# First layer's attention: fp32 operands on the two halves of the tensor engine in place of split ones on all of it

## The chip, the cores and the metric

The kernel runs on one core of a Trainium2 chip. The metric is the device time of one execution in microseconds (us); a kernel's time is the median of several. The engines of a core run side by side, each through its own queue: TensorE (PE; its weight loads are listed as PEld), VectorE (DVE), ScalarE (ACT), GpSimd (POOL), and SyncE (SP), which issues transfers.

## The reference, cut to what matters

The program is three transformer layers over 512 tokens of width 1024; the last ends in a mixture of experts. The change is in the mixer of the first, which runs two kinds of attention, each with 8 heads of width 64, over the same normalized input:

```python
# 'fox': causal, with a decay per head
logits = einsum('bqhd,bshd->bhqs', qb, k) * scale + cq[..., None] - cum_k[:, :, None, :]
p = masked_softmax(logits, causal); out = einsum('bhqs,bshd->bqhd', p, v)
# 'dsa': keys picked by an index score, top 128 of each query
rel = relu(einsum('bqhd,bsd->bqhs', qi, k_idx)); score = einsum('bqhs,bqh->bqs', rel, wi)
_, idx = lax.top_k(score, n_keep)
logits = (q_abs . c_sel + q_rot . kr_sel) * scale
p = masked_softmax(logits, valid); out = (p @ c_sel) @ w_uv
```

Queries go in four blocks i = 0..3 of 128; block i sees keys 0 to (i+1)*128. `n_keep` is min(256, 512 // 4) = 128, so block 0 needs no scores. The kernel holds the dsa keys and values per head, made from `ckv` by w_uk and w_uv, so that both kinds have the same shape of work, the dsa logits with a keep mask in place of the causal one.

## The kernel before, in words

**Precision.** A product that must be nearly fp32 is made of three fp32r passes (`mm3`, L317 to L319: hi*hi, hi*lo, lo*hi). Each operand is split as it leaves PSUM: ACT copies the high part, then DVE subtracts it to get the low one (`split_evac`, L310/L311 and L313/L314). Weights are split in the same way, `whi` by ACT (L267), `wlo` by POOL (L280) or DVE (L282).

**Heads.** Two heads share one [128, 512] tile of transposed queries, one on rows 0 to 63, one on rows 64 to 127. Their keys lie in `kd`, one column block for each head with zeros in the other head's 64 rows (`evac_diag`), so each head's logits are a 128-row product. `P` transposed goes to `PTh` (ACT, L633) and `PTl` (DVE, L637); P times values is `mm3` with 64 columns of values as the weight, 128 columns of P at a time. In the fox heads the decay is added to the logits by one more matmul over 8 rows (L1028).

**Stages of layer 0**, in the order of the program: small projections; the dense product for the index queries; the query product (`dense_T`), whose gaps in the code take the index scores (24 items: three blocks by 8 heads, `idx_item`); the key product and the value product, among whose pieces the 48 top-k rounds on DVE are spread (L975, L976); the product for the dsa queries (`qtok2`); `out_proj`.

**The pipeline.** The attention is 40 items (`softmax_item`), 5 for each of 8 pairs of heads, fox first. `Pipeline.step` emits, for step n, each part of an item by its lag, in the order that `SM0` lists: pv of item n-6, T (transposes, L626) of n-4, max (DVE, L606) of n-1, hi of n-5, norm of n-3, qk of n, lo of n-5, out of n-7, exp of n-2. Each engine runs its queue in that order. Steps 0 to 6 are interleaved with the qtok2 product, steps 7 to 35 stand alone (with a top-k round each at first), the last 11 are interleaved with `out_proj`. The preparation of dsa heads (`prep_pair`, `prep_v`) is hung in ahead of steps 15, 19, 21, 26, 29 and 30.

Of the kernel before, what the change touches and what calls it, by code (L numbers as in the profile page):

```python
# [26 lines left out]
SM0 = [('pv', 6), ('T', 4), ('max', 1), ('hi', 5), ('norm', 3), ('qk', 0), ('lo', 5), ('out', 7), ('exp', 2)]  # L27
# [21 lines left out]
NCOLS = 8  # L49
# [37 lines left out]
def tile_kernel(ctx: ExitStack, tc: tile.TileContext, I, out, stage=None, start=None):  # L87
# [489 lines left out]
    def softmax_items(sched, parts, qk, in1, v, out, gate=None):  # L577

        items = []
        for n, part in enumerate(parts):
            later = {h for p in parts[n + 1:] for h, _ in p}
            items.append(softmax_item(sched, part, qk, in1, v, out, {h for h, _ in part} - later, gate))
        return items

    def softmax_item(sched, segs, qk, in1, v, out, ended, gate, parts=None):
# [9 lines left out]
        def s_qk():  # L598
            st["s"] = ps(128, w)
            qk(st["s"], [(h, i, a) for (h, i), a in zip(segs, at)])  # L600

        def s_max():
            st["nm"] = att.tile([128, 2], F32, tag="nm", name="nm", bufs=4)
            st["p"] = att.tile([128, S], F32, tag="P", name="P", bufs=PBUF)
            for c, ((h, i), a) in enumerate(zip(segs, at)):
                nc.vector.tensor_tensor_reduce(st["p"][:, a], st["s"][:, a], in1(h, i), 1.0, 3e38, ALU.add, ALU.min,  # L606
                                               st["nm"][:, c:c + 1])
# [20 lines left out]
        def s_hi():  # L628
            if parts:
                (nc.vector.tensor_copy if parts[3] else nc.scalar.copy)(parts[0]()[:, :w], st["t"])  # L630
                return
# [7 lines left out]
        def s_pv():  # L639
            if parts:  # L640
                return parts[1]()
            for (h, i), a in zip(segs, at):
                o, empty, use = out(h)
                pv([(h, i)], [a], o(), v, st["h"], st["l"], empty, use is not None)

        def s_out():
            if parts:
                return parts[2]()
            for h in sorted(ended):
                o, _, use = out(h)  # L650
                if use:
                    use(o())

        fs = dict(pv=s_pv, T=s_T, qk=s_qk, hi=s_hi, max=s_max, exp=s_exp, norm=s_norm, lo=s_lo, out=s_out)
# [10 lines left out]
    def qk_pairs(q, k, extra=None):  # L665

        def qk(s, segs):
            for h, i, a in segs:
                w = (i + 1) * 128
                ii = slice(i * 128, w)  # L670
                (qh, ql), (kh, kl) = q(h), k(h)
                mm3(s[:, a], qh[:, ii], ql[:, ii], kh[:, h % 2, :w], kl[:, h % 2, :w], True, extra is None)
                if extra:
                    extra(s[:, a], h, i)
        return qk
# [169 lines left out]
    def layer_0():  # L845
# [13 lines left out]
        kd = []  # L859
        for f in range(4):  # L860
            kd.append(tuple(att.tile([128, 2, S], F32R, name=f"kd{f}{c}") for c in range(2)))
            for a in kd[-1]:
                nc.gpsimd.memset(a[0:64, 1].bitcast(F32), 0.0)
                nc.gpsimd.memset(a[64:128, 0].bitcast(F32), 0.0)
# [29 lines left out]
        dense_tok(352, KD, uh, ul, use_small, begun=begun)  # L894
        def small_T():
            for c in range(2):
                split_evac(ckT[0][:, c], ckT[1][:, c], blocks_T(smt, c * 128), cols[:, C_KV + c:C_KV + c + 1])
            evac_diag(kd[0], blocks_T(smt, 256))
            split_evac(rT[0:16], rT[32:48], blocks_T(smt, 384, 16))
# [3 lines left out]
        ck = att.tile([128, 2, S], F32R, name="ck")  # L903
# [3 lines left out]
        def decay_rows():  # L907
# [16 lines left out]
            for g in range(2):  # L924
                nc.scalar.activation(ck[:, g], cmask, AF.Identity, scale=0.0, bias=cols[:, C_DK + g:C_DK + g + 1])
# [6 lines left out]
            for g in range(2):  # L932
                nc.gpsimd.dma_start(ck[4 * g::32, g], ch[g::2])
                nc.gpsimd.dma_start(ck[4 * g + 1::32, g], cl[g::2])
                nc.gpsimd.dma_start(cq[4 * g + 2::32], nh[g::2])
                nc.gpsimd.dma_start(cq[4 * g + 3::32], nl[g::2])
# [3 lines left out]
        dense_tok(512, KD, uh, ul, rope_tok(qtok), after(1, small_T, decay_rows))  # L940
        qi = []

        def turn_qi():
            qi.append(pair_tiles("q", 4))
            split_evac(*qi[-1], blocks_T(qtok, (len(qi) - 1) * 128))
        score = [None] + [att.tile([128, (i + 1) * 128], F32, name=f"score{i}") for i in (1, 2, 3)]

        def idx_item(i, h):
# [3 lines left out]
            def s_qk():  # L952
                st["s"] = ps(128, w)
                qh, ql = (a[:, i * 128:(i + 1) * 128] for a in qi[h // 2])
                mm3(st["s"], qh, ql, kd[0][0][:, h % 2, :w], kd[0][1][:, h % 2, :w], True, True)

            def s_relu():
                st["r"] = att.tile([128, S], F32, tag="P", name="relu", bufs=PBUF)
                nc.scalar.activation(st["r"][:, :w], st["s"], AF.Relu)

            def s_acc():
                r, sc, wt = st["r"][:, :w], score[i], wi[:, i, h:h + 1]
                if h == 0:
                    nc.vector.scalar_tensor_tensor(sc, r, wt, cmask[:, 512 - w:], ALU.mult, ALU.subtract)
                else:
                    nc.vector.scalar_tensor_tensor(sc, r, wt, sc, ALU.mult, ALU.add)
            return [(0, s_qk), (1, s_relu), (2, s_acc)]

        scoring = Pipeline([idx_item(i, h) for i in (1, 2, 3) for h in range(8)])
# [19 lines left out]
        def some_scores():  # L989
            for _ in range(3):  # L990
# [3 lines left out]
        q_b = []  # L994

        def pair_out(lst, tag, scale, bufs):
            def use(f, p):
                lst.append(pair_tiles(tag, bufs))
                split_evac(*lst[-1], p, scale)
            return use  # L1000

        def v_half():
            return tuple(att.tile([128, NT, 256], F32R, tag="t4", name="v" + s, bufs=T4) for s in "hl")

        dense_T(512, KD, uh, ul, pair_out(q_b, "q", -SCALE, 4),
                fine=after(QF0[0], *[turn_qi] * 4, *[some_scores] * QF0[1]))
        dense_T(512, KD, uh, ul, lambda f, p: evac_diag(kd[f], p), fine=spread_topk(TK0[0]))
        vb = [v_half(), v_half()]

        def v_b(t, p):  # L1010
            for a in range(2):
                split_evac(vb[a][0][:, t], vb[a][1][:, t], p[:, a * 256:(a + 1) * 256])
# [4 lines left out]
        def o_out(f):  # L1017

            def place(h):
                c, hs = f + h // 2, hslice(h)  # L1020
                return lazy(lambda: ps(64)), True, lambda o: split_evac(oT[0][hs, c], oT[1][hs, c], o)
            places = [place(h) for h in range(8)]
            return lambda h: places[h]

        def decay(s, h, i):
            r = slice(h // 2 * 32, h // 2 * 32 + 8)
            w = (i + 1) * 128
# [7 lines left out]
        parts = [[(h + a, i) for a, i in part] for h in range(0, 8, 2) for part in PARTS]  # L1035
        items += softmax_items(SM0, parts, qk_pairs(lambda h: q_b[h // 2], lambda h: kd[h // 2], decay),
                               lambda h, i: cmask[:, 384 - i * 128:], values(vb), o_out(4))


        q_a, va = {}, {}  # L1040
        uk_uv = []

        def prep_pair(f):
            def emit():
                if not uk_uv:
                    uk_uv.append(next_unit(1))
                q_a[f] = pair_tiles("q", 4)
                split_evac(*q_a[f], blocks_T(qtok2, f * 128), -SCALE)
# [5 lines left out]
                evac_diag(kd[f], p)  # L1054
            return emit

        def prep_v(a):
            def emit():
                if len(uk_uv) < 2:
                    uk_uv.append(next_unit(1))  # L1060
                va[a] = v_half()
# [9 lines left out]
        items += softmax_items(SM0, parts, qk_pairs(lambda h: q_a[h // 2], lambda h: kd[h // 2]),  # L1071
                               lambda h, i: keep[i], values(va), o_out(0))
# [6 lines left out]
        while attend.at < len(parts):  # L1079
# [6 lines left out]
                 lambda: [rooms(f"kd{f}{c}", 1, 1)[0] for f in range(2) for c in range(2)], oT)  # L1086
# [3 lines left out]
    def layer_1():  # L1090
# [244 lines left out]
        def halves_mm(o, at, of, start=False, stop=False):  # L1335
# [984 lines left out]
```

## Time and profile before

| | |
|---|---|
| median of 3 runs | 2206.71 us (2206.43 to 2208.38) |
| the profiled execution | 2204.43 us, its span 2202.7 us |
| mean granted TensorE clock | 0.982 |
| PE busy | 2105.9 us, 96% of the span |
| DVE, ACT, POOL busy | 1179.6, 848.6, 437.9 us |
| the stages that the change touches | from 84.9 to about 345 us |

Times in views are us from the first instruction of the profiled execution. The span is from its first to its last instruction; the execution's own time is 1.7 us more. In a row of the timeline the first number is the start, the second the duration; matmuls overlap in the pipeline, so the distance from start to start is what one costs. A granted clock of 1.00 is 2.4 GHz, 0.50 is 1.2 GHz.

### The profile page before, as it was taken

The page shows a single profiled execution, that of the slowest core. Times are in us where ns is not written, and L with a number is a line of the kernel's source. Part 1 is how long each engine was busy: PE and PEld are TensorE (multiplying, and loading weights), DVE is VectorE, ACT ScalarE, POOL GpSimd, SP SyncE. Part 2 cuts the span into 40 slices and gives each one's busy share as a digit, 9 for nine tenths or more (in the row PEclk, how much of TensorE's full clock was granted, in tenths as well). Part 3 has the DMA queues.
Part 4 walks back from the last instruction along what each step waited for, and adds up shares of the span by engine and source line. Part 5 has one row for each costly group of instructions (what it writes and reads, how often), then busy time and mean ns, then how long its engine had stood idle before and what let it go on. Part 6 is the DMA issues. An engine that isn't in the chain of part 4 may idle for free.

```text
span 2202.7 us, 29776 instructions
## 1 busy us (share of the span) xinstructions
PE 2105.9 (96%) x11223; PEld 1569.0 (71%) x11223; DVE 1179.6 (54%) x2385; ACT 848.6 (39%) x1624; POOL 437.9 (20%) x564
## 2 busy tenths in 40 slices
PE   7999999999999989999999999989888999999997
PEld 6877788888888877888888887777767444444443
DVE  5587654588684557734778775563755132212223
ACT  4524663344343356743434444553753010101000
POOL 4333241000001345530000002454353000000000
PEclk9999999999999999999999999999999999999999
DMA  4221022532314210022342322302015999999995
GB/s 133 69 77 49 1 68 77 162 115 86 115 39 122 76 50 2 2 87 92 110 134 68 114 80 72 100 16 86 20 67 212 403 409 409 409 409 409 408 408 204
DMA packets 118835, 328.65 MB, mean 149 GB/s; under 512 B 10604, under 2 KB 12716, under 8 KB 118688
## 3 DMA queue, kind: packets, MB, share of 16 engines
q1 hardware_dynamic: 115888, 318.87, 40.1%
q0 software_dynamic: 2800, 7.84, 1.2%
q8 instruction: 90, 1.47, 0.3%
q14 instruction: 57, 0.47, 0.1%
HBM read 324.49 MB, written 2.11 MB: 148 GB/s over the span
## 4 chain that ended last, share of the span: by engine, by line
PE 55%; DVE 5%; POOL 2%; ACT 1%; issue 1%; DMA 0%; DVEq 0%; POOLq 0%; ACTq 0%
PE ps L2019 16%; PE ps L404 10%; PE ps L347 9%; PE ps L743 5%; PE ps L1990 3%; PE ps L2086 2%; PE ps L1337 2%; PE ps L626 2%; PE ps L1353 2%; DVE sl L1725 1%; POOL wlo L280 1%; PE ps L318 1%; POOL sh L1721 1%; PE ps L319 0%; DVE w L1709 0%
## 5 line engine op out<-in xcount | busy, mean ns | idle before, releaser
L267 ACT ACTIVATE whi<-raw 128x1024 fp32r<-128x1024 f32 (+2 forms) x162 | 168.3, 1042 | 358.5 <-PE ps L404 153.3
L280 POOL TENSOR_TENSOR wlo<-raw,whi 128x512 fp32r<-128x512 f32 (+1 forms) x132 | 169.1, 1303 | 390.6 <-ACT whi L267 362.0
L2019 PE MATMUL ps<-ew,xt 128*64 128x512 f32 x1024 | 229.9, 597 | 0.0
L282 DVE TENSOR_TENSOR wlo<-raw,whi 128x1024 fp32r<-128x1024 f32 (+2 forms) x96 | 116.6, 1215 | 207.3 <-ACT whi L267 207.0
L404 PE MATMUL ps<-oTl,whi 128*128 128x512 f32 (+2 forms) x576 | 211.4, 371 | 1.4 <-DVE oTl L311 1.4
L404 PE MATMUL ps<-oTh,whi 128*128 128x512 f32 (+2 forms) x576 | 211.6, 371 | 0.5 <-ACT oTh L310 0.5
L404 PE MATMUL ps<-oTh,wlo 128*128 128x512 f32 (+2 forms) x576 | 166.6, 370 | 0.0
L2019 PEld LDWEIGHTS ps<-ew,xt 128*64 128x64 f32 x1024 | 69.4, 137 | 128.2 <-issue 118.9
L347 PE MATMUL ps<-whi,uTh 128*128 128x512 f32 (+2 forms) x384 | 152.0, 397 | 5.3 <-ACT uTh L310 3.2
L347 PE MATMUL ps<-whi,uTl 128*128 128x512 f32 (+2 forms) x384 | 147.9, 386 | 2.9 <-DVE uTl L311 2.9
L347 PE MATMUL ps<-wlo,uTh 128*128 128x512 f32 (+2 forms) x384 | 118.9, 388 | 6.4 <-POOL wlo L280 6.2
L404 PEld LDWEIGHTS ps<-oTl,whi 128*128 128x128 f32 x576 | 108.5, 188 | 20.8 <-DVE oTl L311 2.1
L404 PEld LDWEIGHTS ps<-oTh,whi 128*128 128x128 f32 x576 | 108.5, 188 | 19.7 <-ACT oTh L310 1.0
L2019 PE MATMUL ps<-ew,hid 128*64 128x512 f32 x512 | 118.4, 600 | 0.7 <-ACT hid L2039 0.7
L404 PEld LDWEIGHTS ps<-oTh,wlo 128*128 128x128 f32 x576 | 104.8, 188 | 18.7
L694 DVE TENSOR_TENSOR x<-ps,x 128x512 f32<-128x512 f32 x124 | 82.0, 684 | 67.0 <-PE ps L347 40.1
L445 POOL DMA_DIRECT2D room<-gains x5 | 2.9, 574 | 566.5 <-DVE fwlo L289 283.4
L613 ACT ACTIVATE P<-P,nm 128x512 f32<-128x512 f32 (+2 forms) x192 | 106.1, 555 | 11.6 <-DVE nm L606 10.4
L606 DVE CUSTOM_DVE_ANT_0 P<-ps,cst 128x128 f32<-128x128 f32 (+3 forms) x168 | 75.0, 473 | 35.1 <-POOL P L621 17.7
L2067 POOL CAST pick<-cst 32x128 fp32r<-32x128 f32 x16 | 4.9, 307 | 442.5 <-PE ps L2074 442.5
L2029 ACT ACTIVATE silu<-ps 128x512 f32<-128x512 f32 x16 | 9.6, 597 | 212.8 <-PE ps L2019 212.8
L347 PEld LDWEIGHTS ps<-wlo,uTh 128*128 128x128 f32 x384 | 72.7, 193 | 24.1 <-POOL wlo L280 10.8
(553 smaller groups left out, 5002.0 us busy)
## 6 DMA issues: line engine op xcount, KB each, us to landing
ew<-w SPq DMA_DIRECT2D x384, 512.0 KB, 10.2
raw<-mlp_w SPq DMA_DIRECT2D x80, 512.0 KB, 3.8
fraw<-mlp_w SPq DMA_DIRECT2D x48, 512.0 KB, 5.6
raw<-w_in SPq DMA_DIRECT2D x24, 512.0 KB, 3.8
raw<-ab_w_in SPq DMA_DIRECT2D x20, 512.0 KB, 3.6
raw<-c_w_in SPq DMA_DIRECT2D x12, 512.0 KB, 3.6
raw<-ab_w_out SPq DMA_DIRECT2D x8, 512.0 KB, 3.8
raw<-c_w_out SPq DMA_DIRECT2D x8, 512.0 KB, 3.7
```

Of the source, the lines that this page charges most:

```text
L267: nc.scalar.activation(hi[:, :w], raw[:, :w], AF.Copy)
L280: nc.gpsimd.tensor_tensor(lo[:, h], raws[r][:, h], hi[:, h], ALU.subtract)
L282: nc.vector.tensor_tensor(lo[:, :w], raws[r][:, :w], hi[:, :w], ALU.subtract)
L347: nc.tensor.matmul(p, a[:, tt], w[:, k], start=u == 0 and n == 0, stop=u == nk - 2 and n == 5)
L404: nc.tensor.matmul(p[:, tt], w[:, k, ff], b[:, u + k, tt], start=start and n == 0, stop=u == nk - 2 and n == 5, **kw)
L606: nc.vector.tensor_tensor_reduce(st["p"][:, a], st["s"][:, a], in1(h, i), 1.0, 3e38, ALU.add, ALU.min, st["nm"][:, c:c + 1])
L613: nc.scalar.activation(p, p, AF.Exp, scale=-1.0, bias=st["nm"][:, c:c + 1], accum_out=st["sm"][:, c:c + 1])
L626: nc.tensor.transpose(st["t"][:, j:j + 128], st["p"][:, j:j + 128], ident)
L694: nc.vector.tensor_tensor(xs, p, xs, ALU.add)
L743: nc.tensor.matmul(acc[b][t], p[:, 2 * h + k, tt], v[:, k], start=begins and h == 0 and m == 0, stop=m == 5, skip_group_check=True)
L1990: nc.tensor.matmul(v, htok[a][:, t, c * 128:(c + 1) * 128], oo[q][:, t], start=t == 0 and a == 0, stop=t == NT - 1 and a == 1)
L2019: nc.tensor.matmul(p[n][half(b)], xs[:, half(b)], w[b][:, n * 512:n * 512 + 512], start=k == 0, stop=k == nk - 1)
```

## The change

`mm3`, the splits of queries, keys, values and P, and the zero-padded `kd` go out of this attention. Operands are plain fp32 copies. `two_rows` makes the logits of a pair by two fp32 matmuls, one with the 64 rows of each head, into two PSUM banks; the fox decay is added in the same way (`decay`), its rows now spread over the pair's 64-row halves. `two_columns` makes P times values by two fp32 matmuls whose 64 weight columns lie on the two halves of the columns. The index scores go by pairs too: 12 items in place of 24. A pair still takes 5 items, but they are cut otherwise: head 0 and head 1 with block 3, head 0 and head 1 with blocks 2 and 0, both heads with block 1 (`two_heads`); the logits of both heads are emitted with the first head's item, the products with the second's. The copy of transposed P is one copy: on ACT for the first head's items, on DVE for the others; `lo` is gone from `SM0`. The output of a pair is split once, not once for each head.

```diff
-SM0 = [('pv', 6), ('T', 4), ('max', 1), ('hi', 5), ('norm', 3), ('qk', 0), ('lo', 5), ('out', 7), ('exp', 2)]
+SM0 = [('pv', 6), ('T', 4), ('max', 1), ('hi', 5), ('norm', 3), ('qk', 0), ('out', 7), ('exp', 2)]
...
-    def softmax_item(sched, segs, qk, in1, v, out, ended, gate, parts=None):
+    def softmax_item(sched, segs, qk, in1, gate, place, take, use, on_vector):
...
-            st["s"] = ps(128, w)
-            qk(st["s"], [(h, i, a) for (h, i), a in zip(segs, at)])
+            st["s"] = qk(segs, at)
...
-            st["h"], st["l"] = (att.tile([128, S], F32R, tag="PT" + c, name="PT" + c, bufs=3) for c in "hl")
-            nc.scalar.activation(st["h"][:, :w], st["t"], AF.Copy)
-        def s_lo():
-            if not parts:
-                nc.vector.tensor_tensor(st["l"][:, :w], st["t"], st["h"][:, :w], ALU.subtract)
...
+            (nc.vector.tensor_copy if on_vector else nc.scalar.copy)(place()[:, :w], st["t"])
+        fs = dict(pv=take, T=s_T, qk=s_qk, hi=s_hi, max=s_max, exp=s_exp, norm=s_norm, out=use)
...
+    def two_rows(dst, of, start=True, stop=True):
+        for c in range(2):
+            nc.tensor.matmul(dst[c], *of(c, slice(c * 64, c * 64 + 64)), start=start, stop=stop)
+    def two_columns(o, at, of, start=False, stop=False):
+        for c in range(2):
+            nc.tensor.matmul(o[c * 64:c * 64 + 64, at], *of(c), start=start, stop=stop, skip_group_check=True,
+                             tile_position=(0, c * 64))
...
+        def pair_tile(tag, bufs, p, scale=1.0):
+            a = att.tile([128, S], F32, tag=tag, name=tag, bufs=bufs)
+            nc.scalar.activation(a, p, AF.Copy, scale=scale)
+            return a
+        def keys(lst, p):
+            f = len(lst)
+            if f % 2 == 0:
+                room_k.append(att.tile([128, 2, S], F32, tag="kd", name="kd", bufs=4))
+            lst.append(room_k[-1][:, f % 2])
+            nc.scalar.activation(lst[f], p, AF.Copy)
+        room_k = []
...
+                st["s"] = [ps(128, w) for _ in range(2)]
+                two_rows(st["s"], lambda c, r: (qi[f][r, i * 128:w], ki[0][r, :w]))
...
-        dense_T(512, KD, uh, ul, lambda f, p: evac_diag(kd[f], p), fine=spread_topk(TK0[0]))
-        vb = [v_half(), v_half()]
+        dense_T(512, KD, uh, ul, lambda f, p: keys(k_b, p), fine=spread_topk(TK0[0]))
...
+            nc.scalar.copy(vb[t // 2][:, t % 2], p)
...
-        def decay(s, h, i):
-            r = slice(h // 2 * 32, h // 2 * 32 + 8)
-            w = (i + 1) * 128
-            nc.tensor.matmul(s, cq[r, i * 128:w], ck[r, h % 2, :w], start=False, stop=True,
-                             tile_position=(h // 2 * 32, 0))
-        def values(vt):
-            return lambda h, j: tuple(a[:, j, h % 4 * 64:h % 4 * 64 + 64] for a in vt[h // 4])
+        def decay(f, s, i, w):
+            two_rows(s, lambda c, r: (cq[r, i * 128:(i + 1) * 128], ck[r, f, :w]), False)
...
+        def two_heads(f, q, k, extra, in1, v, to):
+            o = lazy(ps)
+            new = lambda: att.tile([128, S], F32, tag="PT", name="PT", bufs=6)
+            nothing = lambda: None
+            out, begun = [], []
+            def logits(part):
+                s = [ps() for _ in range(2)]
+                w = 0
+                for i in part:
+                    n = (i + 1) * 128
+                    dst = [a[:, w:w + n] for a in s]
+                    two_rows(dst, lambda c, r: (q()[r, i * 128:n], k()[r, :n]), stop=extra is None)
+                    if extra:
+                        extra(f, dst, i, n)
+                    w += n
+                return s
+            def products(i, p):
+                for j in range(i + 1):
+                    two_columns(o(), slice(i * 128, i * 128 + 128), lambda c: (v(2 * f + c, j), p(c)[:, j * 128:j * 128 + 128]),
+                                not begun, j == i)
+                    begun.append(1)
+            for part in ((3,), (2, 0)):
+                p = [lazy(new), lazy(new)]
+                s = lazy(lambda part=part: logits(part))
+                def take(p=p, part=part):
+                    for i, at in zip(part, (0, 384)):
+                        products(i, lambda c: p[c]()[:, at:])
+                for c in range(2):
+                    out.append(softmax_item(SM0, [(2 * f + c, i) for i in part], lambda segs, at, s=s, c=c: [s()[c][:, a] for a in at],
+                                            in1, None, p[c], take if c else nothing, nothing, c))
+            p = lazy(new)
+            out.append(softmax_item(SM0, [(2 * f, 1), (2 * f + 1, 1)], lambda segs, at: [a[:, 0:256] for a in logits((1,))], in1, None, p,
+                                    lambda: products(1, lambda c: p()[:, c * 256:]),
+                                    lambda: split_evac(oT[0][:, to + f], oT[1][:, to + f], o()), 1))
+            return out
...
-                    split_evac(va[a][0][:, t], va[a][1][:, t], p)
+                    (nc.vector.tensor_copy if t % 2 else nc.scalar.copy)(va[t // 2][:, t % 2, a * 256:(a + 1) * 256], p)
```

What the engines' queues hold, in the program's order. First PE before, in the steps that stand alone, one fox step with blocks 2 and 0 and the start of the next step's work (`kd` keys, `qh`, `ql` queries, `PT` transposed P, `cst` the identity):

```order
L626 MATMUL ps<-cst,P 128x128 x4
L317 MATMUL ps<-kd_279,qh 128x384
L318 MATMUL ps<-kd_280,qh 128x384
L319 MATMUL ps<-kd_279,ql 128x384
L1028 MATMUL ps<-ck,cq 128x384
L317 MATMUL ps<-kd_279,qh 128x128
L318 MATMUL ps<-kd_280,qh 128x128
L319 MATMUL ps<-kd_279,ql 128x128
L1028 MATMUL ps<-ck,cq 128x128
L317 MATMUL ps<-PTh,vh 64x128
L318 MATMUL ps<-PTl,vh 64x128
L319 MATMUL ps<-PTh,vl 64x128
```

Now the five steps of one pair of heads at the same place:

```order
L614 MATMUL ps<-cst,P 128x128 x4
L638 MATMUL ps<-PT,v 64x128 x8
L614 MATMUL ps<-cst,P 128x128 x4
L633 MATMUL ps<-kd,q 128x384 x2
L633 MATMUL ps<-ck,cq 128x384 x2
L633 MATMUL ps<-kd,q 128x128 x2
L633 MATMUL ps<-ck,cq 128x128 x2
L614 MATMUL ps<-cst,P 128x128 x4
L638 MATMUL ps<-PT,v 64x128 x8
L614 MATMUL ps<-cst,P 128x128 x4
L633 MATMUL ps<-kd,q 128x256 x2
L633 MATMUL ps<-ck,cq 128x256 x2
```

Before, each step holds logits, products and transposes; now two of five steps hold transposes alone, and the products of both heads stand together ahead of the next logits. DVE at the same place, now (L594 is the row maximum, `nm` its result):

```order
L594 ISA P,nm<-ps,cst 128x384
L594 ISA nm 128x1
L594 ISA P,nm<-ps,cst 128x128
L594 ISA nm 128x1
L617 COPY PT<-ps 128x512
L606 RECIPROCAL sm<-sm 128x1
L594 ISA P,nm<-ps,cst 128x384
L594 ISA nm 128x1
L594 ISA P,nm<-ps,cst 128x128
L594 ISA nm 128x1
L617 COPY PT<-ps 128x512
```

Before, each step's maximum was followed by the subtraction for `PTl`; now in three of five steps by a copy that makes all of a transposed P. In two of the three, as in the first copy here, the maximum ahead of it is that of the item whose logits PE gets in the step before. The scoring on PE, now, among rows of the query product:

```order
L633 MATMUL ps<-ki,q 128x256 x4
L404 MATMUL ps<-uTh,whi 128x512
L404 MATMUL ps<-uTl,whi 128x512
L404 MATMUL ps<-uTh,whi 128x512
L404 MATMUL ps<-uTl,whi 128x512
L404 MATMUL ps<-uTh,wlo 128x512 x2
L633 MATMUL ps<-ki,q 128x384 x4
```

Each row of `ki,q` is two items, a pair of matmuls each; before there were nine rows of `mm3`, three items, at each such place.

## Rows read from the trace of the kernel before

**Rows 1.** Stretches: us, busy PE, PEld, DVE, ACT, POOL, clock, DMA share, GB/s.

```profile
84.90:107.10 22.20, 22.20 (x115) 19.41 (x114) 15.92 (x24) 12.62 (x25) 2.73 (x2) 1.00 0.16 48
...
135.70:163.70 28.00, 25.42 (x97) 19.80 (x96) 22.79 (x53) 9.39 (x14) 10.12 (x8) 0.88 0.26 76
163.70:195.30 31.60, 30.64 (x143) 22.40 (x142) 23.68 (x70) 14.06 (x34) 13.20 (x16) 1.00 0.23 67
195.30:209.00 13.70, 13.69 (x112) 10.62 (x112) 13.53 (x42) 8.58 (x23) 5.98 (x11) 1.00 0.11 40
209.00:239.60 30.60, 29.09 (x217) 22.97 (x217) 17.56 (x54) 15.69 (x43) 6.78 (x14) 0.94 0.01 1
239.60:287.60 48.00, 44.08 (x390) 39.37 (x391) 32.99 (x98) 33.40 (x86) 14.06 (x26) 0.96 0.01 1
```

**Rows 2.** PE's waits from 0 to 420 us: total, times, longest.

```profile
PE ps L347 <- POOL wlo L280: 5.8, 8, 1.2
PE ps L318 <- DVE PTl L637: 4.1, 4, 1.3
```

**Rows 3.** PE's timeline at the key product's end.

```profile
137.83 0.50 PE L347 MATMUL ps<-whi,uTh 128*128 128x512 f32 x1 [1.97 <-ACT whi L267]
```

**Rows 4.** ACT's timeline there.

```profile
134.04 1.21 ACT L310 ACTIVATE kd<-ps 64x512 fp32r<-64x512 f32 x2 [7.06 <-DVE kd L311]
```

**Rows 5.** PE's timeline in the index scores.

```profile
102.04 0.39 PE L319 MATMUL ps<-kd,ql 128*128 128x512 f32 x1
102.27 0.39 PE L317 MATMUL ps<-kd,qh 128*128 128x512 f32 x1
```

**Rows 6.** PE's timeline in a dsa step.

```profile
282.28 0.63 PE L626 MATMUL ps<-cst,P 128*128 128x128 f32 x4
282.67 0.48 PE L317 MATMUL ps<-kd,qh 128*128 128x512 f32 x1
...
283.44 0.22 PE L317 MATMUL ps<-PTh,vh 128*64 128x128 f32 x1
...
284.15 0.41 PE L626 MATMUL ps<-cst,P 128*128 128x128 f32 x2
```

**Rows 7.** PE's timeline in a fox step.

```profile
205.13 0.40 PE L319 MATMUL ps<-kd,ql 128*128 128x512 f32 x1
205.46 0.49 PE L1028 MATMUL ps<-ck,cq 8*128 8x512 f32 x1
205.88 0.27 PE L317 MATMUL ps<-PTh,vh 128*64 128x128 f32 x1
```

**Rows 8.** PE's timeline: four fp32 matmuls, all rows and columns.

```profile
1393.20 3.60 PE L1492 MATMUL ps<-hankel,jm 128*128 128x512 f32 x8
1396.24 0.79 PE L347 MATMUL ps<-whi,uTh 128*128 128x512 f32 x1
```

**Rows 9.** PE's timeline: fp32 pairs on column halves, layer 1.

```profile
853.33 1.08 PE L1337 MATMUL ps<-pcT,vcs 128*64 128x512 f32 x4
854.24 1.04 PE L1337 MATMUL ps<-PT,vsw 128*64 128x128 f32 x16
855.21 0.66 PE L626 MATMUL ps<-cst,P 128*128 128x128 f32 x4
```

**Rows 10.** DVE's timeline in a fox step.

```profile
206.02 0.68 DVE L975 MAX8 m<-score 128x8 f32<-128x512 f32 x1
...
207.41 0.68 DVE L606 CUSTOM_DVE_ANT_0 P<-ps,cst 128x512 f32<-128x512 f32 x1
...
208.09 0.67 DVE L637 TENSOR_TENSOR PTl<-ps,PTh 128x512 fp32r<-128x512 f32 x1
```

**Rows 11.** DVE's copies of P, layer 1: ns min/median/max.

```profile
L630 DVE COPY PT<-ps x40: 668/685/692, 815.3 to 949.7; 128x512 f32<-128x512 f32 x40
```

**Rows 12.** Busy time behind two of PE's stalls; columns of rows 1.

```profile
248.00:250.00 2.00, 2.00 (x16) 2.00 (x17) 1.97 (x7) 1.35 (x5) 0.53 (x2) 0.56 0.00 0
...
264.00:266.00 2.00, 1.91 (x23) 1.71 (x21) 1.91 (x8) 1.92 (x5) 0.25 (x1) 1.00 0.00 0
```

More of the change, by code (lines that the diff above doesn't have):

```diff
@@ L923, in decay_rows @@
             nc.scalar.activation(cq, cmask, AF.Copy, scale=0.0, bias=1.0)
-            for g in range(2):
-                nc.scalar.activation(ck[:, g], cmask, AF.Identity, scale=0.0, bias=cols[:, C_DK + g:C_DK + g + 1])
+            rows_k.append(att.tile([128, S], F32R, tag="ckall", name="ckall"))
+            nc.scalar.activation(rows_k[0], cmask, AF.Identity, scale=0.0, bias=cols[:, C_DK:C_DK + 1])
             ch = att.tile([8, S], F32R, tag="P", name="ch", bufs=PBUF)
@@ L932, in decay_rows, with decay_keys, idx_item @@
             for g in range(2):
[L933 to L936, printed above, removed]
+                for n, (dst, src) in enumerate(((rows_k[0], ch), (rows_k[0], cl), (cq, nh), (cq, nl))):
+                    nc.gpsimd.dma_start(dst[64 * g + n:64 * g + 16:4], src[g::2])
+        def decay_keys():
+            for f in range(4):
+                nc.scalar.activation(ck[:, f], rows_k[0], AF.Copy, scale=cols[:, C_DK + 1 + f:C_DK + 2 + f])
         qtok = []
-        dense_tok(512, KD, uh, ul, rope_tok(qtok), after(1, small_T, decay_rows))
+        dense_tok(512, KD, uh, ul, rope_tok(qtok), after(1, small_T, decay_rows, decay_keys))
         qi = []
         def turn_qi():
-            qi.append(pair_tiles("q", 4))
-            split_evac(*qi[-1], blocks_T(qtok, (len(qi) - 1) * 128))
+            qi.append(pair_tile("q", 8, blocks_T(qtok, len(qi) * 128)))
         score = [None] + [att.tile([128, (i + 1) * 128], F32, name=f"score{i}") for i in (1, 2, 3)]
-        def idx_item(i, h):
+        def idx_item(i, f):
             w = (i + 1) * 128
@@ L1034, in layer_0 @@
         items = []
[L1035 to L1040, printed above, removed]
+        for f in range(4):
+            items += two_heads(f, lambda f=f: q_b[f], lambda f=f: k_b[f], decay, lambda h, i: cmask[:, 384 - i * 128:],
+                               lambda h, j: vb[j // 2][:, j % 2, h * 64:h * 64 + 64], 4)
@@ L1041, in layer_0 @@
+        q_a, k_a, va = {}, [], []
         uk_uv = []
@@ L1053, in emit @@
                 nc.tensor.matmul(p, ekr[0:48], rT[0:48], start=False, stop=True)
-                evac_diag(kd[f], p)
+                keys(k_a, p)
             return emit
@@ L1085, in layer_0 @@
         out_proj(*([a[:, k] for k in order] for a in oT), attend,
-                 lambda: [rooms(f"kd{f}{c}", 1, 1)[0] for f in range(2) for c in range(2)], oT)
+                 lambda: rooms("kd", 4, 4), oT)
     def layer_1():
@@ L1331, in layer_1 @@
         ol = big.tile([128, KD, S], F32R, tag="Tl", name="oTl")
-        def halves_mm(o, at, of, start=False, stop=False):
-            for c in range(2):
-                nc.tensor.matmul(o[c * 64:c * 64 + 64, at], *of(c), start=start, stop=stop, skip_group_check=True,
-                                 tile_position=(0, c * 64))
         def started(f):
             o = ps()
-            halves_mm(o, slice(0, S), lambda a: (vcs[f // 4][:, f % 2 * 2 + a], pcT[:, f // 2, :]), start=True)
+            two_columns(o, slice(0, S), lambda a: (vcs[f // 4][:, f % 2 * 2 + a], pcT[:, f // 2, :]), start=True)
             return o
@@ L1347, in ended, with qk @@
             nc.vector.tensor_tensor(ol[:, f], o, oh[:, f], ALU.subtract)
-        def qk(s, segs):
-            for n, i, a in segs:
+        def qk(segs, at):
+            s = ps(128, at[-1].stop)
+            for (n, i), a in zip(segs, at):
                 h, w = n // 2, (i + 1) * 128
@@ L1369, in items @@
                 for a in range(2):
-                    out.append(softmax_item(SM1, segs(a), qk, lambda n, i: cmask[:, 384 - i * 128:], None, None, None,
+                    out.append(softmax_item(SM1, segs(a), qk, lambda n, i: cmask[:, 384 - i * 128:],
                                             lambda n, i: gate[:, i, n // 2 * 3 + 1 + n % 2:n // 2 * 3 + 2 + n % 2],
-                                            (p[a], (lambda: take(p)) if a else nothing, use if a else nothing, a)))
+                                            p[a], (lambda: take(p)) if a else nothing, use if a else nothing, a))
             for part in ((3,), (2, 0)):
```

117 lines of the change are left out of this document (36 added, 81 removed).

## The prediction, made before the changed kernel ran

> **What bounds the kernel now.** I read the busy time by stretch first, because the share of the whole span (PE 96%) says nothing of a stage. The change touches six stretches [rows 1]: the query product with the index scores (84.9 to 107.1), the key and value products with their ends (135.7 to 163.7 holds the second half), pipeline steps 0 to 6 inside the qtok2 product (163.7 to 195.3), steps 7 to 11 (to 209.0), 12 to 19 (to 239.6) and 20 to 35 (to 287.6); the last 11 steps lie in `out_proj`. In all but one PE is busy for nearly all of its time, and where it is not, the other engines are far from full too: it waits. The exception is 195.3 to 209.0: DVE is busy for 13.53 of 13.70 us there, with a top-k round in each step. So PE's work is worth its time nearly everywhere, and a saving on PE in steps 7 to 11 only what DVE saves.
>
> PE's waits come next. It stands 5.8 us for `wlo` in eight waits and 4.1 us for `PTl` in four [rows 2], and 1.97 us for `whi` at the end of the key product [rows 3]. That last one is ACT: it stood 7.06 us for DVE in the `kd` splits [rows 4], because DVE works off top-k rounds ahead of each subtraction, and `whi` of the next product is queued behind the splits. Behind such a wait the granted clock falls: 0.88 over 28.0 us [rows 1]; behind a 1.2 us wait for `PTl` it was 0.56 in 248 to 250, behind another 1.00 [rows 12]. A stall thus costs its length and sometimes about 2 us more.
>
> **What PE work costs, before and after.** Passes of 512 columns follow each other 0.23 us apart [rows 5]. A dsa step spends 0.77 on three of them, with what the change of shape costs, 0.71 on twelve passes of products, and 0.39 on transposes [rows 6]. A pair of heads has 2 x 1280 columns of logits: three passes, 3.45 us at 0.23 per 512, and 0.08 in each of five steps, 3.9. Its products are 60 passes of 0.059, 3.55. A fox head adds the decay: 0.42 from its start to the next row, and 0.10 more on the pass ahead of it (0.33 instead of 0.23), 0.52 [rows 7]; by 0.23 per 512 columns the eight of a pair come to 2 x (0.52 + 0.46 + 0.40 + 0.35), 3.5.
>
> After: four fp32 matmuls of 512 columns on the whole array take 3.04 to the next start and 3.60 to their own end [rows 8], 0.76 to 0.90 each; I take 0.86. A pair on two column halves takes 0.91, with the change of shape (853.33 to 854.24), so it costs about what one costs; four pairs of 128 columns take 0.97, 0.243 each [rows 9]. Products of a pair of heads are ten such: 2.45, **1.1 less**. No row shows two fp32 matmuls on row halves. If they overlap as the column halves do, the logits of a pair cost 0.86 x 1280 / 512 = 2.14, with the changes of shape 2.4, **1.5 less**; if they take turns, 4.3. I take the first, since the nearest row is the one with two halves of this same array and this same type. The decay as fp32r pairs is then 1280 columns, 0.58, **2.9 less**. A dsa pair saves 2.6, a fox pair 5.5.
>
> The Trainium skill ("TensorE: Matmul & The Clock Gate", Part 3, "Measured speedup vs the span model") gives four tiles on the rows a speedup of 3.07, not 4, and three on the columns 2.38. The trace's column pair is nearer to a full overlap (0.91 against 0.86); of rows it shows nothing. By the page's ratio a row pair would take about 1.3 times one matmul, which is the second rival.
>
> **What the new order makes late.** Now P of the second head goes through DVE, behind the maximum of the item whose logits were just made. PE reaches the products and waits: maximum 0.68, copy 0.69 [rows 10, 11], an estimated 0.27 for the hand-overs between engines, less one set of transposes, 0.39: about 1.25 us, twice per pair (ahead of each pair's eight products). Behind that wait stand the next transposes and logits. In steps 0 to 6 and in the last 11 the dense product fills it; in steps 12 to 35 a preparation hung in at that place fills about half. That leaves three in 12 to 19 and three in 20 to 35. Against it the old waits for `PTl` at the preparations go, as queries, keys and values need one copy each and no subtraction behind DVE's queue.
>
> **The sum, by stretch** (us saved):
> - Index scores: 8 heads x 3 passes x (0.23 + 0.173 + 0.117), 12.4, against 4 pairs x (0.86 + 0.64 + 0.43), 7.7, and six places with a change of shape at 0.2: **3.5**. ACT and DVE do the same number of operations; DVE has 15.92 of 22.2 us, so it hardly binds.
> - End of the key product: 1.97 and some 0.6 more of waits, and 28.0 x (1 - 0.88) = 3.4 of clock; four copies on ACT replace eight split halves, so `whi` comes in time. I take **5.5** of 6.0.
> - End of the value product: the longest wait for `wlo`, 1.2 [rows 2], was queued behind the same splits: **1.2**.
> - Steps 0 to 6: logits and decay of 1.4 pairs, 1.4 x 4.4 = 6.2; **5.5**, since DVE's top-k rounds may leave gaps that the dense product doesn't fill.
> - Steps 7 to 11: DVE loses five subtractions and one output split (0.68 each), gains three copies: 2.0 at most, 0 if new waits eat it: **1.0**.
> - Steps 12 to 19: 1.6 fox pairs, 8.8; an old wait of 1.3 and 30.6 x 0.06 = 1.8 of clock; less 3 x 1.25 and 2 for the clock behind them: 11.9 - 5.75, **6.2**.
> - Steps 20 to 35: 3.2 dsa pairs, 8.3; old waits 2.8, clock 48.0 x 0.04 = 1.9; less 3 x 1.25 and 2: **7.3**.
> - Last steps, in `out_proj`: products of two pairs and logits of 0.8, 3.4, less 0.4 for weights that may not be ready sooner: **3.0**.
> The memsets of `kd` on POOL, the four ACT copies of decay rows and the decay's transfers lie in the small projections' stretch beside PE work; if they had no cover they would cost some 2.4 us at 0.6 each (half of the 1.21 in rows 4), which is in the range. Behind layer 0 nothing changes, and PE is the bound until the mixture of experts, so the saving passes through.
>
> Together 33.2: the profiled 2204.4 becomes 2171.2. The median of the runs lies 2.3 above that execution, so the forecast for the median is **2173**. Its own range is 2161 to 2183: the stretches' terms with and without the six stalls (7.5) and the allowance for the clock (4).
>
> **The rivals.**
> 1. *The clock stays low between the stalls.* Steps 7 to 35 are 5.8 pairs, some 11 stalls if preparations fill none; at 2 us each for the clock, and five more stalls than I counted, 22 + 6 - 4 = 24 more at worst, half of that likely: about 2185. For it: the 0.56 in rows 12; against it the 1.00 there behind a similar stall.
> 2. *Row halves overlap in part*, a pair at 1.3 times one: 0.3 x 2.14 x 8 pairs = 5.1, and 0.3 x 7.7 = 2.3 in the scores: 2180.
> 3. *Row halves take turns.* 2.14 x 8 = 17.1, 7.7 in the scores, 0.58 x 4 = 2.3 in the decay: 27.1 more, about 2200, somewhat less (2194) where the longer logits lie under DVE's stretch and the stalls. For it: no row shows an overlap on rows; against it the column rows.
> 4. *Slower.* Row halves take turns, and every change between shapes drains the array for long. At the decay, the only partial row shape in the trace, a change in and out cost 0.10 and 0.19 [rows 7]. There are some nine changes per pair and twelve in the scores, 84; at 0.3 in place of the 0.1 counted that is 17 more: 2173 + 27 + 17 = 2217. It decides from about 0.23 per change on, and only with rival 3.
> 5. *No change that can be measured*: rival 3 and half of rival 4, or a stall of POOL or ACT in `out_proj` as large as the saving; no row speaks for one.
>
> **Chances.** Forecast 0.55; rival 1 0.15, rival 2 0.12, rival 3 0.10, rival 4 0.05, rival 5 0.03. A measurement of this kernel can tell some 0.2%, 4.4 us, from no change. Faster: the first four, 0.92; same 0.03; slower 0.05. The range reaches down to 2159, where no unfilled stall and no low clock is left and DVE gives its 2.0, and up to 2196, into rival 3; outside lie half of it, rivals 4 and 5, and a small tail below.
>
> **What would show it.** In the trace after: pairs at `two_rows` with 512 columns 0.86 to 0.95 from start to start of what follows (1.7 if they take turns); four products in 1.0; the scores' stretch 3.5 shorter; no 1.97 us wait for `whi` behind the keys; new waits of PE for `PT` from DVE, near 1.25 us each, about six long ones in steps 12 to 35; a granted clock below 1.00 there. I am wrong if the row pairs cost twice as much, if the waits for `PT` come in every pair and the clock stays near 0.6 between them, or if a wait in the dense products takes the place of the one for `whi`.

## The result

The changed kernel takes 2170.52 us (median of four, 2170.16 to 2172.74) where the kernel before took 2206.57 (median of four, 2206.43 to 2208.38): 0.9837 of it, 95% interval 0.982 to 0.9854. The profiled execution has a span of 2168.5 us, 34.2 less than before. On the page of its profile TensorE's share has not changed; it is still by far the busiest engine.

```profile
PE 2076.8 (96%) x10975; PEld 1527.3 (70%) x10975; DVE 1141.0 (53%) x2319; ACT 824.7 (38%) x1578; POOL 428.2 (20%) x548
```

Busy time by stretch, columns as in rows 1: scores; value product and the first pieces of qtok2; steps 0 to 6, 7 to 11, 12 to 19, 20 to 35; the steps in `out_proj` with the product. These are the stretches of the changed kernel.

```profile
84.17:102.57 18.40, 18.40 (x85) 10.86 (x85) 13.64 (x20) 11.45 (x24) 2.71 (x2) 1.00 0.18 48
127.08:162.50 35.42, 35.42 (x157) 29.10 (x155) 29.00 (x68) 10.41 (x13) 14.48 (x12) 1.00 0.35 102
162.50:177.57 15.07, 15.07 (x80) 10.32 (x79) 9.63 (x36) 7.73 (x21) 5.93 (x8) 1.00 0.21 71
177.57:191.03 13.46, 11.07 (x85) 7.45 (x84) 12.72 (x46) 7.21 (x22) 7.94 (x14) 0.87 0.12 39
191.03:214.03 23.00, 21.27 (x183) 15.67 (x182) 12.66 (x48) 11.70 (x34) 7.20 (x14) 1.00 0.01 2
214.03:254.56 40.53, 38.99 (x303) 25.84 (x301) 22.13 (x78) 25.59 (x72) 15.16 (x27) 1.00 0.00 1
254.56:308.36 53.80, 53.74 (x306) 41.69 (x305) 19.44 (x55) 22.28 (x48) 23.79 (x28) 1.00 0.35 108
```

And the kernel before, cut at the same instructions where rows 1 were cut otherwise:

```profile
130.26:173.70 43.44, 39.90 (x157) 30.90 (x156) 35.75 (x81) 14.07 (x22) 14.34 (x12) 0.92 0.29 82
...
195.24:209.00 13.76, 13.75 (x113) 10.68 (x112) 13.56 (x42) 8.58 (x23) 6.04 (x11) 1.00 0.11 40
209.00:239.60 30.60, 29.09 (x217) 22.97 (x217) 17.56 (x54) 15.69 (x43) 6.78 (x14) 0.94 0.01 1
239.60:287.30 47.70, 43.78 (x389) 39.12 (x390) 32.70 (x98) 33.09 (x85) 13.77 (x25) 0.96 0.01 1
287.30:344.04 56.74, 55.70 (x355) 47.09 (x354) 24.53 (x61) 28.02 (x60) 24.72 (x28) 1.00 0.33 103
```

| saved, us | forecast | measured |
|---|---|---|
| ahead of the scores (start at 84.91, now 84.17) | 0 | 0.7 |
| scores to the value product (45.35, now 42.91) | 3.5 | 2.4 |
| value product to the first logits (43.44, now 35.42) | 5.5 + 1.2 | 8.0 |
| steps 0 to 6 (21.5, now 15.1) | 5.5 | 6.5 |
| steps 7 to 11 | 1.0 | 0.3 |
| steps 12 to 19 | 6.2 | 7.6 |
| steps 20 to 35 | 7.3 | 7.2 |
| the last steps, with `out_proj` | 3.0 | 2.9 |
| sum | 33.2 | 35.6 |

At 308 us the changed kernel leads by 35.7; 1.5 is lost between 720 and 740 us, at the start of layer 1, which the change doesn't touch. The same waits stand there in both kernels, but behind them the granted clock fell to 0.83 in this execution.

How the row pairs run shows in the scores, in TensorE's timeline: two pairs of 512 columns (four matmuls, two records each) between dense passes.

```profile
95.08 0.62 PE L404 MATMUL ps<-uTh,wlo 128*128 128x512 f32 x2
95.64 1.99 PE L633 MATMUL ps<-ki,q 64*128 64x512 f32 x8
97.55 0.50 PE L404 MATMUL ps<-uTh,whi 128*128 128x512 f32 x1
97.89 0.40 PE L404 MATMUL ps<-uTl,whi 128*128 128x512 f32 x1
```

Four fp32 matmuls in 1.91 us, what two of 0.86 [rows 8] and a change of shape take: the halves work at the same time. The price by length says the same: two pairs of 384 columns take 1.50 us (89.45 to 90.95), so 0.41 buys 256 columns more, 0.82 per 512, no more than a matmul on the whole array costs. The change of shape itself costs more than the forecast's 0.2 per place: 0.11 ahead (0.56 where two passes take 0.45), 0.2 within, 0.11 on the pass behind (0.34 for 0.23), 0.4 in all.

TensorE's waits from 60 to 330 us (total, times, longest) have two new rows in place of those in rows 2:

```profile
PE ps L638 <- DVE PT L617: 3.2, 6, 0.6
PE ps L614 <- POOL P L609: 2.3, 1, 2.3
```

### The profile page after: what moved, and what is told of

Its sections match the earlier page's. It is cut to its first block, busy times and chain, and to the rows that moved or that the text cites. A ratio compares the mean times of both kernels' runs of the same rounds, so it can differ in the third digit from the quotient of the medians.

```text
span 2168.5 us, 29075 instructions
## 1 busy us (share of the span) xinstructions
PE 2076.8 (96%) x10975; PEld 1527.3 (70%) x10975; DVE 1141.0 (53%) x2319; ACT 824.7 (38%) x1578; POOL 428.2 (20%) x548
## 4 chain that ended last, share of the span: by engine, by line
PE 56%; DVE 5%; POOL 2%; ACT 2%; issue 1%; DMA 0%; POOLq 0%; DVEq 0%; ACTq 0%
PE ps L2019 16%; PE ps L404 10%; PE ps L347 8%; PE ps L707 5%; PE ps L1990 3%; PE ps L2086 2%; PE ps L638 2%; PE ps L614 2%; PE ps L1352 2%; POOL wlo L280 1%; PE ps L318 1%; DVE sl L1725 1%; PE ps L319 0%; POOL sh L1721 0%; PE ps L317 0%
## 5 line engine op out<-in xcount | busy, mean ns | idle before, releaser
L601 ACT ACTIVATE P<-P,nm 128x384 f32<-128x384 f32 (+2 forms) x192 | 106.2, 557 | 22.2 <-DVE nm L594 19.1
L594 DVE CUSTOM_DVE_ANT_0 P<-ps,cst 128x128 f32<-128x128 f32 (+3 forms) x168 | 74.9, 473 | 37.9 <-POOL P L609 18.6
```

Source lines behind the costliest of these rows:

```text
L594: nc.vector.tensor_tensor_reduce(st["p"][:, a], st["s"][c], in1(h, i), 1.0, 3e38, ALU.add, ALU.min, st["nm"][:, c:c + 1])
L601: nc.scalar.activation(p, p, AF.Exp, scale=-1.0, bias=st["nm"][:, c:c + 1], accum_out=st["sm"][:, c:c + 1])
```

## The experiments

Ratios are to the kernel before on the same chip, with 95% intervals; stretches are from each kernel's profile. e1 to e10 name the runs. "Scores to normalization" is the time from the first score to the first transpose of the next layer's normalization: 259.13 us before, 224.19 in the changed kernel.

**Both matmuls of a row pair on the same rows (e1).** The second head's logits and scores are those of the first, so the output is not the reference's.

```diff
-            nc.tensor.matmul(dst[c], *of(c, slice(c * 64, c * 64 + 64)), start=start, stop=stop)
+            nc.tensor.matmul(dst[c], *of(c, slice(0, 64)), start=start, stop=stop)
```

> The changed kernel with both matmuls of each row pair (logits, decay, index scores) on rows 0 to 63: the second head's logits and scores are those of the first, the number and size of all instructions stays. Theory: the changed kernel's gain on the logits comes from the two row halves working at the same time. Then each pair here costs two matmuls: 2.14 us more per pair of heads, 17.1 for eight, 7.7 in the scores, 2.3 in the decay, 27 in all, 2 to 4 of it hidden where VectorE sets the pace; 2193 to 2198 us, and two pairs of 512 columns take about 3.6 us where they took 1.91. Rival: the gain comes from fewer passes and from the splits that went, and the halves matter little: 2170 to 2174 us.

Measured: scores to normalization 252.07, 27.9 more than the changed kernel; 7.7 of that in the scores' part (50.59 against 42.91). The whole kernel took 2338.98 us (1.0596, 1.0575 to 1.0618), because the changed values sent more tokens to some expert than fit and a second loop of the mixture (L2180 to L2209, absent from the other traces) ran; up to the router the trace is 29.7 later than the changed kernel's. In TensorE's timeline the two score pairs of 512 columns, which took 1.91 there:

```profile
99.79 3.70 PE L633 MATMUL ps<-ki,q 64*128 64x512 f32 x8
103.42 0.50 PE L404 MATMUL ps<-uTh,whi 128*128 128x512 f32 x1
```

3.63 for the same instructions, as forecast: on the same rows they take turns. The theory holds and its price, 27, was right; without the row halves the change would have saved about 8.

**Products on one column half (e2).** `o` is two banks, and the output is split per head as before the change.

```diff
-                    two_columns(o(), slice(i * 128, i * 128 + 128), ...
+                    one_half(o(), slice(i * 128, i * 128 + 128), ...
...
+            nc.tensor.matmul(o[c][:, at], *of(c), start=start, stop=stop, skip_group_check=True)
```

> The changed kernel with the products of both heads on the same 64 columns, each head into its own PSUM bank, and the output split per head as before the change. Theory: column halves overlap, so undoing them makes 10 pairs of 0.243 us cost twice: 2.4 us per pair of heads, 19 for eight, less 2 to 4 where VectorE sets the pace: 2186 to 2190 us. Rival: at 64 weight columns and 128 moving columns the weight loads are what bounds these products, and the halves give little: 2171 to 2176 us.

Measured: 2186.37 us (0.9905, 0.9886 to 0.9923), scores to normalization 238.66, 14.5 more than the changed kernel. A set of eight products in TensorE's timeline:

```profile
223.21 1.96 PE L644 MATMUL ps<-PT,v 128*64 128x128 f32 x16
225.10 0.66 PE L614 MATMUL ps<-cst,P 128*128 128x128 f32 x4
```

1.89 us where the changed kernel takes 1.03 (219.26 to 220.29): the column halves overlap too, and the rival falls. By these rows 2.5 such sets in each of eight pairs cost 17.2 us; one pair's 2.1 of that shows nowhere, because steps 7 to 11 took 13.33 us here (177.52 to 190.85) against 13.46 in the changed kernel: VectorE paces them, as the theory allowed. The remaining 0.6 was not followed.

**Copy of P ahead of the maximum (e3).**

```diff
-SM0 = [('pv', 6), ('T', 4), ('max', 1), ('hi', 5), ('norm', 3), ...
+SM0 = [('pv', 6), ('T', 4), ('hi', 5), ('max', 1), ('norm', 3), ...
```

> The changed kernel with the copy of transposed P ahead of the row maximum in the pipeline's order. Theory: the six waits of TensorE for PT (0.55 to 0.63 us each, with the gap ahead of them some 0.85) are there because the copy stands behind the maximum of logits just made; they go, and nothing takes their place, since P is needed two steps after the maximum: 5 us less, 2165 to 2167 us. Rival: the later maximum makes the exponential and the normalization late, and the wait moves to the transposes (for P from GpSimd): 2169 to 2172 us.

Measured: 2166.62 us (0.9819, 0.9801 to 0.9838), scores to normalization 220.31, 3.9 less. The waits for `PT` fell from 3.2 to 0.3 us; those for `P` from GpSimd rose from 2.3 to 3.9:

```profile
PE ps L614 <- POOL P L609: 3.9, 6, 1.7
...
PE ps L638 <- DVE PT L617: 0.3, 1, 0.3
```

Both theories have a part in it: the waits for `PT` were due to the order, and for the 2.9 us of them that went, 1.6 us of waits for `P` came at the transposes. The time is in the theory's range, the saving short of its 5 us.

**Copy and reciprocal ahead of the maximum (e6).** In `SM0`, `('hi', 5), ('norm', 3), ('max', 1)` follow each other.

> The copy-first order with the normalization's reciprocal ahead of the row maximum too. Theory: the waits for P from GpSimd that the copy-first order brought (3.9 us in six, with the one of 1.7) come from reciprocals that stand behind a maximum on VectorE; they shrink by 1 to 2 us: 2164.5 to 2166 us. Rival: what is late there is GpSimd behind the weight split or VectorE full of top-k rounds: no change, 2166 to 2168 us.

Measured: 2164.93 us (0.9809, 0.9794 to 0.9824), scores to normalization 218.12, another 2.2 less; the wait for `P` is one of 1.3 us. The theory holds.

**Five top-k rounds earlier (e4).** `TK0 = (20, 14, 9)` becomes `(20, 14, 14)`.

> The changed kernel with the last five top-k rounds moved from steps 7 to 11 into the qtok2 product. Theory: the stretch of steps 7 to 11 (13.46 us in the changed kernel, TensorE busy for 11.07 at a clock of 0.87) is bound by VectorE with its five rounds (1.4 us each); without them it falls to 10 or 11 us: 2167 to 2168 us. Rival: its length is set by the wait of 2.25 us for P from GpSimd, which stands behind the split of a weight unit, and by the clock that falls behind it: it shortens by less than 1 us, and the rounds may make the product before it longer: 2170 to 2172 us.

Measured: 2170.59 us (0.9839, 0.9823 to 0.9856): no change. Steps 7 to 11 took 13.14 us with VectorE busy for 7.07 us, where they had taken 13.46 with VectorE busy for 12.72:

```profile
177.59:190.73 13.14, 10.70 (x85) 7.11 (x84) 7.07 (x32) 7.21 (x22) 8.09 (x14) 0.87 0.12 40
```

The rival is right: without the rounds something else holds this stretch at nearly the same length. It stands in the changed kernel's own timeline too, GpSimd first, then TensorE, then the clock behind:

```profile
178.96 2.50 POOL L280 TENSOR_TENSOR wlo<-raw,whi 128x512 fp32r<-128x512 f32 x2
181.42 0.87 POOL L534 TENSOR_TENSOR qtok<-ra,rb 128x128 f32<-128x128 f32 x2
182.27 0.93 POOL L609 TENSOR_SCALAR P<-P,sm 128x256 f32<-128x256 f32 x2
```

```profile
182.80 0.89 PE L614 MATMUL ps<-cst,P 128*128 128x128 f32 x4 [2.25 <-POOL P L609]
183.62 2.77 PE L638 MATMUL ps<-PT,v 128*64 128x128 f32 x16
```

```profile
184.00:186.00 2.00, 1.88 (x16) 1.57 (x14) 1.97 (x6) 0.68 (x4) 0.69 (x1) 0.50 0.25 95
```

The normalization of P waits on GpSimd behind a weight split and the rope; TensorE stands for 2.25 us, its clock falls to 0.50 (1.2 GHz), and eight products take 2.70 us where they take 1.03 elsewhere (219.26 to 220.29).

In the changed kernel itself, though, VectorE is still full beside all this; first these 12 us, then steps 7 to 11 of its second execution (e10, below), in which TensorE stood just as long and the clock stayed at 1.00:

```profile
178.61:190.61 12.00, 9.61 (x67) 6.33 (x66) 11.83 (x41) 6.17 (x20) 6.90 (x11) 0.86 0.14 44
```

```profile
182.46 0.89 PE L614 MATMUL ps<-cst,P 128*128 128x128 f32 x4 [2.24 <-POOL P L609]
```

```profile
177.24:190.32 13.08, 9.84 (x85) 6.37 (x85) 12.33 (x46) 7.43 (x22) 7.94 (x14) 1.00 0.13 40
```

With the clock up the stretch was only 0.4 us shorter. So two limits of about the same length lie here: VectorE's queue with its rounds, and GpSimd's queue with the clock behind it. Taking the first away uncovers the second. Taking away the second alone was not tried.

**The weight split on VectorE, with the rounds earlier (e7).**

```diff
-VEC = {'attn0': (0, 3, 10, 12, 22, 27, 31), ...
+VEC = {'attn0': (0, 3, 10, 12, 22, 25, 27, 31), ...
```

> The changed kernel with the last five top-k rounds moved into the qtok2 product, as in e4, and the low half of the weight unit that GpSimd splits at 179 us now made by VectorE. Theory: the wait of 2.25 us for P at step 8 is there because GpSimd works off this split (2.5 us) first, and the clock of 0.5 behind it follows from that wait; without them steps 7 to 11 take 10 to 11 us where they took 13.4: 2167 to 2168 us. Rival: the split takes 1.24 us on VectorE and the rope of the dsa queries stays, so that the wait moves to VectorE's maximum: 2169 to 2171 us.

Measured: steps 7 to 11 took 11.0 us and kept their clock; the kernel 2169.55 us (0.9833, 0.9818 to 0.9848).

```profile
177.78:188.80 11.02, 9.19 (x85) 6.15 (x84) 7.74 (x33) 7.09 (x22) 6.69 (x12) 1.00 0.14 48
```

```profile
182.04 0.93 POOL L609 TENSOR_SCALAR P<-P,sm 128x256 f32<-128x256 f32 x2 [0.57 <-DVE sm L606]
```

In the second row GpSimd, now free, waits for VectorE's reciprocal, which stands behind the split, the rope and a maximum; TensorE still waits 1.8 us for `P`. So most of the wait moved to VectorE, as the rival had it, but the clock did not fall behind it, and the stretch is 2.1 us shorter than with the rounds alone: 0.6 is the wait (2.42 there, 1.8 here), the other 1.5 TensorE's busy time (10.70, now 9.19), which is the clock. Since the clock also stayed up behind 2.24 us in the changed kernel's second execution, this trace does not show that the moved split kept it up. The median moved by less, within the spread of the runs.

**All three together (e8).**

> All three orders together: copy and reciprocal ahead of the maximum, the five top-k rounds earlier, the weight unit's low half on VectorE. Theory: the waits stand in different steps, so that the savings add up: some 5 us from the order, 3 from steps 7 to 11: 2161 to 2164 us. Rival: in steps 7 to 11 they are the same saving, and the whole is that of the order alone: 2165 to 2167 us.

Measured: 2162.18 us (0.9798, 0.9784 to 0.9811), faster than both kernels; scores to normalization 214.99, 9.2 less than the changed kernel. Steps 7 to 11:

```profile
177.61:187.73 10.12, 9.21 (x86) 6.16 (x85) 8.23 (x33) 7.20 (x22) 5.80 (x12) 1.00 0.19 53
```

The savings add up (6.1 for the order and 2.2 for the weight split with the rounds, each alone; 0.9 more together), and no wait for `PT` is left. The slowest of its runs (2162.93) is faster than the fastest with the order alone (2164.31), so the rounds and the split together do pay.

**Subtractions of the fox keys put back (e5).** The differences are stored and not used.

```diff
+                for c in range(2):
+                    cs = slice(c * 64, c * 64 + 64)
+                    nc.scalar.activation(lst[f][cs], p[cs], AF.Copy)
+                    nc.vector.tensor_tensor(low[cs], p[cs], lst[f][cs], ALU.subtract)
```

> The changed kernel with the fox keys leaving PSUM as before the change: each 64-row half copied by ScalarE and subtracted by VectorE (the difference is stored and not used). Theory: the 8.0 us that the changed kernel saves between the start of the value product and the first attention step came from this chain alone, in which ScalarE waited for VectorE behind top-k rounds and the weight copy behind it came late. Then the wait for whi near 2 us and the lower clock come back: 5 to 8 us more, 2175 to 2179 us. Rival: the saving came from the values, which have one copy for each token block now and no subtraction; then at most 2 us come back, 2170 to 2173 us.

Measured: 2174.15 us (0.9849, 0.9834 to 0.9864); value product to first logits 38.01, 2.6 more. The wait for `whi` came back, 0.8 us long, and the clock did not fall. That lies between the two: the keys alone bring back a third of the 8.0 us.

**Subtractions of queries, keys and values put back (e9).** The same for `q_b` (128x512) and for the values (two halves of 256 columns).

> The changed kernel with the fox queries, keys and values all leaving PSUM with VectorE's subtractions as before the change (the differences are stored and not used). Theory: the saving of 8.0 us between the start of the value product and the first attention step came from these three; the keys alone brought 2.6 us of it back without a fall of the clock. With the queries' subtractions VectorE reaches the keys some 1.2 us later, the wait for whi comes back to 2 us, and the values bring 1 to 2 us more: 4.5 us without the clock, up to 8 us with it, in that stretch; 2175 to 2179 us. Rival: the rest of the 8.0 us is elsewhere (the order of transfers or weight splits); the stretch stays within 1 us of that with the keys alone, 38.0 us.

Measured: 2181.23 us (0.9889, 0.9872 to 0.9905); value product to first logits 44.67, 9.2 more than the changed kernel and 1.2 more than the kernel before. ScalarE's timeline, then TensorE's:

```profile
131.81 1.21 ACT L839 ACTIVATE kd<-ps 64x512 f32<-64x512 f32 x2 [8.24 <-DVE low L840]
```

```profile
135.60 0.80 PE L347 MATMUL ps<-whi,uTh 128*128 128x512 f32 x1 [3.15 <-ACT whi L267]
```

```profile
126.86:171.53 44.67, 39.52 (x158) 30.54 (x156) 36.98 (x84) 14.04 (x22) 14.47 (x12) 0.92 0.28 80
```

This is the chain of rows 3 and 4, and at 0.92 the clock of before: 44.67 x 0.08 = 3.6 of the 9.2 is the clock's. The theory holds, though the stretch went past its 8 us and the median past its 2179. The values' part shows by itself, at the end of the value product:

```profile
161.68 0.50 PE L347 MATMUL ps<-whi,uTh 128*128 128x512 f32 x1 [1.01 <-ACT whi L267]
```

With two waits for `wlo` behind it (0.17 and 0.73) that is 1.9 us, none of it in the run with the keys alone. The queries' subtractions were not tried by themselves; but the wait of 3.15 us comes before the first value is copied (151.18 on ScalarE), so the values have no part in it, and what it has over the 0.8 with the keys alone goes to the queries.

**The changed kernel again (e10).**

> The changed kernel once more, beside the one with the splits on the same chip, to see which parts of its profile vary by themselves: 2169 to 2173 us; the stretches of layer 0 within 0.5 us of the first profile, the fall of the clock behind the waits of layer 1's start there or not.

Measured: 2169.3 us (0.9835, 0.9818 to 0.9852), span 2166.4; scores to normalization 224.07 against 224.19. Single waits vary more: those for `PT` are eight with 4.2 us here where they were six with 3.2. In layer 1 the clock did not fall this time. The changed kernel's first profile, then this one, at that place:

```profile
724.30:734.30 10.00, 7.74 (x31) 6.37 (x30) 3.80 (x16) 2.68 (x5) 6.53 (x10) 0.83 0.36 104
```

```profile
724.00:734.00 10.00, 7.75 (x38) 6.43 (x37) 4.57 (x20) 3.62 (x7) 7.25 (x12) 1.00 0.36 104
```

TensorE is busy alike in both and did fewer instructions in the first. The 1.5 us that the changed kernel seemed to give back there is the clock's doing in one execution, not the change's.

## Why the prediction was right

The forecast of 2173 us was 2.5 above the median, within its own range, for the reasons given; some of its terms were off in ways that cancelled.

- **Row halves overlap.** Taken from the column row [rows 9], as no row showed them. The changed kernel's scores and the run on the same rows settle it: 27.9 us lie in it, and rivals 2, 3 and 4 fall. The ratio of 3.07 for four row tiles, which the Trainium skill gives ("TensorE: Matmul & The Clock Gate", Part 3, "Measured speedup vs the span model"), did not carry over to two halves: a pair took the time of one.
- **Changes of shape** were mis-sized: 0.2 per place in the scores, measured 0.4. That is 1.2 of the scores' term (3.5, measured 2.4). In the steps four transposes ahead of a change take 0.59 where they took 0.39 [rows 6].
- **The new waits** stood where forecast: six in steps 12 to 35, for `PT` from VectorE. In the changed kernel's timeline:

```profile
190.44 0.66 PE L614 MATMUL ps<-cst,P 128*128 128x128 f32 x4
191.03 0.43 PE L638 MATMUL ps<-PT,v 128*64 128x128 f32 x2
192.01 1.09 PE L638 MATMUL ps<-PT,v 128*64 128x128 f32 x14 [0.55 <-DVE PT L617]
```

  The first head's product starts, the second's waits for its copy: 0.98 us for what takes 0.12, so about 0.86 and not 1.25 (no row had given the 0.27 for the hand-overs in it), and the clock stayed at 1.00 there, where 4 us had been allowed for it. Some 6 us too much in steps 12 to 35; the changes of shape, with some ten per pair at 0.1 more than counted in 4.8 pairs, take about 5 of it back, an estimate from the 0.59 above. Hence 7.6 and 7.2 for 6.2 and 7.3. Rival 1 did not come.
- **Steps 7 to 11** gave 0.3 for 1.0. That VectorE paces them was right: it is busy for 11.83 of 12.00 us there. But its list was incomplete. Eight operations of the dsa queries' rope, 1.3 us, which had ended ahead of step 7 in the kernel before, now fall into this stretch. The forecast also did not see the second limit close behind, GpSimd's queue and the clock, which leaves moving the five rounds without effect.
- **The end of the key and value products** gave 8.0 for 6.7: TensorE, busy for 39.90 of 43.44 us before, now never stands there. The 1.2 was misread: the longest wait for `wlo` of rows 2 stands at 31.93, far ahead of these products, and at the value product's end is one of 0.73, as the kernel before's timeline shows:

```profile
31.93 0.43 PE L347 MATMUL ps<-wlo,uTh 128*128 128x352 f32 x1 [1.16 <-POOL wlo L280]
...
166.54 0.50 PE L347 MATMUL ps<-wlo,uTh 128*128 128x512 f32 x1 [0.73 <-POOL wlo L280]
```

  The chain from the keys to `whi` was right, but not all its causes: the keys' subtractions alone bring back 2.6, and only with the queries' as well does VectorE come late enough for a wait of 3.15 us, behind which the clock fell; the values' cost 1.9 further on. The queries' part was not in the sum at all.
- **The 0.7 us ahead of the scores** was not foreseen, and its cause was not tried. Much of it may be chance: in the eleven traces of the changed kernel and its variants the scores start between 83.93 and 84.66.

## What to carry to other kernels

Two K = 64 or M = 64 products on the halves of the array cost what one costs, so three fp32r passes over a half-empty array lost here to one fp32 pair; count the changes of shape, at 0.4 us for each block that stands alone among full ones. When work on TensorE shrinks, look at what each queue holds ahead of the operation that now ends last: here another order of the pipeline's parts, five top-k rounds moved and one weight split on another engine were worth 8.3 us more. Where two limits are nearly equal, lifting one shows nothing. A subtraction on a loaded engine costs what waits behind it on the next one, not its own length.

## What the runs showed of the hardware

The granted clock fell behind some waits and not behind others of like length. In steps 7 to 11 of the changed kernel it fell to 0.50 behind 2.25 us in one execution and stayed at 1.00 behind 2.24 in another; in the same place it fell behind 1.31 us with copy and reciprocal first (0.87 over 177.51 to 190.40) and not behind 1.82 with the weight split moved. Behind the same waits at the start of layer 1 it fell in one execution of the changed kernel and not in the other. That fall cost 1.5 us, as much as the smaller terms of the sum, so single profiles differ by that much; the one in steps 7 to 11 cost 0.4, since VectorE was the next limit there.
